# Post-normed products with tokens in the rows: TensorE transposes four blocks ahead of the next products, and four tiles of these run side by side

## The chip, the cores and the metric

One core of one Trainium2 chip runs the whole program. The metric is the device time of one execution in microseconds (us), lower is better; three executions of the kernel before gave a median of 1262.53 us (1261.92 to 1263.29). One more execution was profiled; the rows of the trace are from that one.

## The reference

256 tokens of width 1024 go through two transformer blocks. Only the first block is touched by the change. Cut to what matters:

```python
def first_block(x, mem, ...):
    h = rmsnorm(x, norm_pre_mix)
    z = h @ w_in
    out_a = gmlp_spatial_gating(g_u, g_v, ...)
    out_b = forgetting_attention(f_q, f_k, f_v, log_f)
    out_c = memory_cross_attention(m_q, rmsnorm(mem, norm_mem), w_mem_kv)
    y = concatenate([out_a, out_b, out_c]) @ w_out
    x = x + rmsnorm(y, norm_post_mix)
    h = rmsnorm(x, norm_pre_ffn)
    f = square(relu(h @ w_ff1)) @ w_ff2
    x = x + rmsnorm(f, norm_post_ffn)
    return x

def second_block(x, ...):
    for i in range(2):
        x = x + 0.5 * swiglu(rmsnorm_2(x, ffn_norm1[i]), wg, wu, wd)
        ...
```

The two lines that matter have the form `x = x + rmsnorm(product, gain)`. They are post-norms: the product's root mean square over all 1024 features must be known before any of it can be added to x. The next layer's products need that x. So each of these lines stands between two long runs of matrix products: `w_out` and `w_ff1` in the one case (called the mix transition here), `w_ff2` and the first swiglu's `wg`, `wu` in the other (the feed-forward transition).

## The kernel before, in words

Activations lie transposed: x is eight tiles `x0` to `x7` of 128 features x 256 tokens. Every fp32 product is made of three fp32r matmuls: each operand is split into a rounded part and a rest (`xh`, `xl` for activations, `wh`, `wl` for weights), and `mm_t` (lines 134 to 141) adds `xh*wh` (line 139), `xl*wh` (line 140) and `xh*wl` (line 141) into one PSUM tile. The weight block is the stationary operand, 256 tokens are the moving one, so one output tile of 128 features x 256 tokens from 1024 inputs takes 8 x 3 = 24 matmuls of 256 columns. `mm_n` (lines 143 to 151) does the same with the activations stationary.

The order of work is written out by hand; each engine runs its own list in the order of the program. The class `Stream` (lines 72 to 131) brings the weights: SyncE's queue issues the DMAs of 1 MB into three `raw` tiles, ScalarE rounds a chunk of 1024 columns to `wh` (line 102), VectorE makes the rest `wl` (line 112). There are six pairs of `wh`, `wl`; `get()` keeps four chunks ahead, so a chunk's pair is reused six chunks later.

The mix transition before (lines 796 to 823): the gating of the first mixer part is finished (lines 796 to 809: 12 small matmuls at line 801, VectorE line 804, GpSimd line 808, split lines 212 and 213). `out_proj` makes `y = w_out` product in tiles of 128 features; `y_evac` (lines 483 to 492) squares each on ScalarE, adds the squares up on GpSimd (line 199) and writes `y` times the gain. After the last tile, `norm_cols` (lines 223 to 229) sums the squares over features with matmuls against ones (line 219); VectorE (line 226) and GpSimd (a power of -0.5, line 188) give the factor of each token; since tokens lie in the columns, `diag` (line 234) and a matmul against ones (line 239) spread it over the partitions. `ws.fill()` (lines 126 to 129) splits two more weight chunks in between, the rest of one of them on GpSimd. `post_add` (lines 531 to 546) multiplies and adds the tiles of x one by one (533, 535, two adds on VectorE and six on GpSimd), rounds `xh` on ScalarE (536) and makes `xl` on VectorE (543). Four blocks of small bf16 matmuls for the position bias of a later layer (`t5_mm`, line 522, 24 matmuls each) are put between these steps. Then `ff1` starts with two tiles whose matmuls alternate by input block (lines 846 to 850).

The feed-forward transition before (lines 877 to 899) has the same parts, with the squared norm folded into the factor (lines 888 to 894). It is followed by `ffn2` (lines 388 to 439), whose first tiles run one after another, and whose `start` (lines 925 to 933) makes the squares for the next norm. Steps of the bias (`t5_mask`: GpSimd line 513, VectorE line 515; `t5_evac`: VectorE line 528) are spread over the tiles of `ffn2` as `extra`.

Of the kernel before, what the change touches and what calls it, by code (L numbers as in the profile page):

```python
# [39 lines left out]
N_HOT = 10  # L40

# [9 lines left out]
def block_kernel(ctx: ExitStack, tc: tile.TileContext, a: dict, out: bass.AP, upto: int = 99):  # L51
# [20 lines left out]
    class Stream:  # L72
# [53 lines left out]
        def fill(self):  # L126

            while self.ns < self.ng + HL and self.split(gp):
                pass

# [12 lines left out]
    def mm_n(ps, w, off, n, x, tt, kts, first, last):  # L143
        h, lo = w
        ts = slice(tt * P, tt * P + P)
        for j, (k, kk) in enumerate(kts):
# [4 lines left out]
            pe.matmul(ps, lhsT=x[0][k][:, ts], rhs=lo[:, c:c + n], start=False, stop=s1)  # L151

# [235 lines left out]
    def ffn2(acc, gnext, extra=(), start=None, more=()):  # L388
        extra = list(extra)
        with tc.tile_pool(name="ffa", bufs=1) as fa, tc.tile_pool(name="fft", bufs=2) as ft:  # L390
# [12 lines left out]
            w, w2 = ws.get(), ws.get()  # L403
            p0, p1 = bank(), bank()
            lo7, hi = range(KT - 1), [KT - 1]
            mm_t(p0[:, :T], w, 0, P, X, lo7, True, False)
            mm_t(p1[:, :T], w2, 0, P, X, lo7, True, False)
            if start:
                start()
            mm_t(p0[:, :T], w, 0, P, X, hi, False, True)  # L410
            mm_t(p1[:, :T], w2, 0, P, X, hi, False, True)
            p2 = bank()
            mm_t(p2[:, :T], ws.get(), 0, P, X, range(KT), True, True)
            ms, rs = norm_cols(acc, *more)
            mm_t(p2[:, T:], ws.get(), 0, P, X, range(KT), True, True)
            rb = bcast(rs)
            evac(0, p0[:, :T], p1[:, :T], rb)
            evac(1, p2[:, :T], p2[:, T:], rb)
            for j in range(2, 22):
# [63 lines left out]
    def y_evac(d, p, y, yacc, gi):  # L483

        if d == KT - 1:
            sq = tp.tile([P, T], F32, tag="sq", name="sq")
            act.activation(out=sq, in_=p, func=AF.Square)
        else:
            sq = None
            add_sq(yacc, d, p)  # L490
        act.activation(out=y[d], in_=p, func=AF.Copy, scale=gcol(gi, d))
        return sq
# [38 lines left out]
    def post_add(y, rb, gnext):  # L531
        def add(d):
            dve.tensor_tensor(out=y[d], in0=y[d], in1=rb, op=ALU.mult)
            eng = dve if d < 2 else gp
            eng.tensor_tensor(out=x[d], in0=x[d], in1=y[d], op=ALU.add)
            act.activation(out=xh[d], in_=x[d], func=AF.Copy, scale=gcol(gnext, d))  # L536
            late.append((d, gcol(gnext, d)))

        for d in range(KT):
            add(d)  # L540
            if d > 1:
# [924 lines left out]
```

## Time and profile before

| what | value |
|---|---|
| median of three executions | 1262.53 us (1261.92 to 1263.29) |
| the profiled execution | 1259.43 us |
| span in its trace | 1257.6 us |
| PE (TensorE matmul) busy | 1222.9 us, 97% |
| VectorE (DVE) busy | 846.2 us, 67% |
| ScalarE (ACT) busy | 660.1 us, 52% |
| GpSimd (POOL) busy | 196.1 us, 16% |
| mean granted TensorE clock | 0.989 of full |

The profiled execution took 1259.43 us, of which 1257.6 us are the span of the trace and 1.8 us lie around it. Matmuls are pipelined, so the time of one (0.28 us for 256 columns) is longer than the distance between two that follow each other, and a share of 97% doesn't mean that TensorE is at its peak. Where a stage's work is read, the start of one row is taken from the start of a later one.

### The profile page before, as it was taken

The page shows a single profiled execution, that of the slowest core. Times are in us where ns is not written, and L with a number is a line of the kernel's source. Part 1 is how long each engine was busy: PE and PEld are TensorE (multiplying, and loading weights), DVE is VectorE, ACT ScalarE, POOL GpSimd, SP SyncE. Part 2 cuts the span into 40 slices and gives each one's busy share as a digit, 9 for nine tenths or more (in the row PEclk, how much of TensorE's full clock was granted, in tenths as well). Part 3 has the DMA queues.
Part 4 walks back from the last instruction along what each step waited for, and adds up shares of the span by engine and source line. Part 5 has one row for each costly group of instructions (what it writes and reads, how often), then busy time and mean ns, then how long its engine had stood idle before and what let it go on. Part 6 is the DMA issues. An engine that isn't in the chain of part 4 may idle for free.

```text
span 1257.6 us, 24874 instructions
## 1 busy us (share of the span) xinstructions
PE 1222.9 (97%) x10316; PEld 1187.9 (94%) x10316; DVE 846.2 (67%) x1490; ACT 660.1 (52%) x1174; POOL 196.1 (16%) x192
## 2 busy tenths in 40 slices
PE   8989999999899999999999999999999989999998
PEld 7878899999899999988999999999999869999998
DVE  6886676654677656688766656666566797666553
ACT  5557465444335544577554444545444787545442
POOL 5424210110420001121200001100001462000000
PEclk9999899999899999999999999999999999999999
DMA  7534355655235545631465455555456412555463
GB/s 239 195 104 165 102 201 179 224 193 179 99 132 178 194 153 193 225 135 64 173 202 194 156 183 203 200 171 202 170 170 201 168 68 92 177 193 181 156 203 108
DMA packets 37266, 211.38 MB, mean 168 GB/s; under 512 B 4768, under 2 KB 8224, under 8 KB 18848
## 3 DMA queue, kind: packets, MB, share of 16 engines
q1 hardware_dynamic: 37152, 209.78, 48.9%
q8 instruction: 81, 1.33, 0.4%
q14 instruction: 33, 0.27, 0.1%
HBM read 208.71 MB, written 1.05 MB: 167 GB/s over the span
## 4 chain that ended last, share of the span: by engine, by line
PE 83%; DVE 9%; issue 3%; ACT 2%; DMA 1%; POOL 1%; SPq 0%; ACTq 0%; POOLq 0%; DVEq 0%
PE ps L139 26%; PE ps L140 26%; PE ps L141 25%; DVE wl L112 3%; PE ps L300 1%; PE ps L311 1%; PE ps L332 1%; DMA raw<-in_w1q 1%; PE ps L149 1%; PE ps L150 1%; ACT wh L102 1%; PE ps L151 1%; DVE p L289 1%; ACT p L271 0%; DVE dg L234 0%
## 5 line engine op out<-in xcount | busy, mean ns | idle before, releaser
L139 PE MATMUL ps<-xh,wh 128*128 128x256 f32 (+1 forms) x1848 | 522.0, 282 | 0.5 <-ACT xh L536 0.5
L140 PE MATMUL ps<-xl,wh 128*128 128x256 f32 (+1 forms) x1848 | 519.6, 281 | 1.5 <-DVE xl L543 0.8
L112 DVE TENSOR_TENSOR wl<-raw,wh 128x1024 fp32r<-128x1024 f32 (+3 forms) x434 | 488.7, 1166 | 47.4 <-ACT wh L102 46.9
L141 PE MATMUL ps<-xh,wl 128*128 128x256 f32 (+1 forms) x1848 | 517.9, 280 | 2.5 <-DVE wl L112 2.5
L102 ACT CAST wh<-raw 128x1024 fp32r<-128x1024 f32 (+4 forms) x436 | 400.4, 959 | 63.8 <-PE ps L140 29.7
L140 PEld LDWEIGHTS ps<-xl,wh 128*128 128x128 f32 (+1 forms) x1848 | 348.9, 189 | 3.5 <-DVE xl L543 2.2
L139 PEld LDWEIGHTS ps<-xh,wh 128*128 128x128 f32 (+1 forms) x1848 | 349.3, 189 | 2.8 <-issue 1.7
L141 PEld LDWEIGHTS ps<-xh,wl 128*128 128x128 f32 (+1 forms) x1848 | 349.1, 189 | 2.8 <-DVE wl L112 2.7
L139 PE MATMUL ps<-ah,wh 128*128 128x256 f32 x960 | 267.8, 279 | 0.0
L140 PE MATMUL ps<-al,wh 128*128 128x256 f32 x960 | 267.8, 279 | 0.0
L141 PE MATMUL ps<-ah,wl 128*128 128x256 f32 x960 | 267.8, 279 | 0.0
L139 PEld LDWEIGHTS ps<-ah,wh 128*128 128x128 f32 x960 | 180.4, 188 | 0.0
L140 PEld LDWEIGHTS ps<-al,wh 128*128 128x128 f32 x960 | 180.4, 188 | 0.0
L141 PEld LDWEIGHTS ps<-ah,wl 128*128 128x128 f32 x960 | 180.4, 188 | 0.0
L199 POOL TENSOR_TENSOR acc<-acc,sq 128x256 f32<-128x256 f32 x42 | 49.9, 1189 | 577.6 <-ACT sq L198 577.4
L398 ACT ACTIVATE s<-t 128x256 f32<-128x256 f32 x88 | 36.8, 418 | 191.8 <-DVE t L396 191.8
L396 DVE TENSOR_TENSOR t<-ps,rb 128x256 f32<-128x256 f32 x88 | 37.2, 423 | 73.4 <-PE ps L141 68.1
L213 DVE TENSOR_TENSOR al<-f,ah 128x256 fp32r<-128x256 f32 (+1 forms) x105 | 49.0, 467 | 52.8 <-ACT ah L212 52.8
L212 ACT CAST ah<-f 128x256 fp32r<-128x256 f32 (+1 forms) x105 | 45.9, 437 | 55.8 <-DVE f L400 43.2
L252 ACT ACTIVATE xh<-x,cols 128x256 fp32r<-128x256 f32 x40 | 20.4, 510 | 101.6 <-DVE x L433 94.6
L400 DVE TENSOR_TENSOR f<-ps,s 128x256 f32<-128x256 f32 x88 | 37.4, 425 | 47.4 <-ACT s L398 47.4
L432 DVE SCALAR_TENSOR_TENSOR t<-ps,rb 128x256 f32<-128x256 f32 x32 | 13.6, 425 | 76.9 <-PE ps L141 76.9
(277 smaller groups left out, 1276.3 us busy)
## 6 DMA issues: line engine op xcount, KB each, us to landing
raw<-in_gu SPq DMA_DIRECT2D x88, 1024.0 KB, 4.9
raw<-in_dn SPq DMA_DIRECT2D x64, 704.0 KB, 4.2
raw<-in_ff SPq DMA_DIRECT2D x32, 1024.0 KB, 4.9
raw<-in_w_out SPq DMA_DIRECT2D x4, 1024.0 KB, 4.8
raw<-in_aq SPq DMA_DIRECT2D x4, 1024.0 KB, 4.7
raw<-in_a_out SPq DMA_DIRECT2D x4, 1024.0 KB, 4.8
raw<-in_b_out SPq DMA_DIRECT2D x4, 1024.0 KB, 4.9
raw<-in_w1q SPq DMA_DIRECT2D x6, 512.0 KB, 3.9
```

The costliest lines, as they stand in the source:

```text
L102: act.copy(h[:, :n], t)
L112: eng.tensor_tensor(out=lo, in0=t, in1=h.bitcast(F32), op=ALU.subtract)
L139: pe.matmul(ps, lhsT=h[:, c:c + m], rhs=x[0][k], start=s0, stop=False)
L140: pe.matmul(ps, lhsT=h[:, c:c + m], rhs=x[1][k], start=False, stop=False)
L141: pe.matmul(ps, lhsT=lo[:, c:c + m], rhs=x[0][k], start=False, stop=s1)
L199: gp.tensor_tensor(out=acc, in0=acc, in1=sq, op=ALU.add)
L212: act.copy(h, src)
L213: dve.tensor_tensor(out=lo, in0=src, in1=h.bitcast(F32), op=ALU.subtract)
L252: act.activation(out=xh[k], in_=x[k], func=AF.Copy, scale=gcol(g, k))
L396: dve.tensor_tensor(out=t, in0=g, in1=rb, op=ALU.mult)
L398: act.activation(out=s, in_=t, func=AF.Silu)
L400: dve.tensor_tensor(out=f, in0=u, in1=s, op=ALU.mult)
```

## The change

In the two post-normed products the roles are exchanged: the activations are stationary, the weights are the moving operand in pieces of 512 columns, and the product lies with tokens in the rows (`mm_y`). The sum of squares of a token is then a sum along the free axis, which ScalarE gives with its accumulator (`y_sq`), and the factor is one scalar per partition (`y_rstd`), which ScalarE (tokens 0 to 127) and VectorE (tokens 128 to 255) multiply on while they bring the product out of PSUM (`y_scale`). TensorE transposes blocks of 128 features back into PSUM, one VectorE instruction multiplies by the gain and adds to x, and `prep` rounds (`PostAdd.turn`). `PostAdd.products` runs four tiles of the next layer's products side by side: for each input block k, two more blocks are transposed (until all eight are), then 12 matmuls use block k. `fill`, the spreading matmul of the factor, GpSimd's adds to x and the sums of squares over tiles on GpSimd go. In the mix transition the gating (12 small matmuls and what follows) moves behind the first three input blocks of the `w_out` product. The squares for the next norm are made in `turn`; `ffn2` takes the four tiles as `begun`, and makes its next factor's diagonal on ScalarE instead of VectorE.

```diff
+MIX_ORDER = [3, 4, 5, 6, 7, 0, 1, 2]
-        def fill(self):
-            while self.ns < self.ng + HL and self.split(gp):
-                pass
+    def mm_y(banks, w, n, x, kts, first, last):
+        for tt in range(2):
+            for j in range(len(banks[tt])):
+                h, lo = w
+                ts = slice(tt * P, tt * P + P)
+                for i, k in enumerate(kts):
+                    c = (i * len(banks[tt]) + j) * n
+                    s0, s1 = first and i == 0, last and i == len(kts) - 1
+                    ps = banks[tt][j][:, :n]
+                    pe.matmul(ps, lhsT=x[0][k][:, ts], rhs=h[:, c:c + n], start=s0, stop=False)
+                    pe.matmul(ps, lhsT=x[1][k][:, ts], rhs=h[:, c:c + n], start=False, stop=False)
+                    pe.matmul(ps, lhsT=x[0][k][:, ts], rhs=lo[:, c:c + n], start=False, stop=s1)
...
+    def y_sq(ps, ss, tt, h, junk):
+        act.activation(out=junk, in_=ps, func=AF.Square, accum_out=ss[:, h, tt:tt + 1])
+    def y_rstd(ss, eps):
...
+        dve.scalar_tensor_tensor(out=ms, in0=ss[:, 1], scalar=1.0 / D, in1=s0, op0=ALU.mult, op1=ALU.add)
+        rs = sm.tile([P, 2], F32, tag="rs", bufs=3, name="rs")
+        rstd_pow(rs, ms, 2)
+        return rs
+    def y_scale(ps, y, rs, pieces):
+        for h, o, n in pieces:
+            src = [ps[tt][h][:, o:o + n] for tt in range(2)]
+            dst = [y[tt][:, 512 * h + o:512 * h + o + n] for tt in range(2)]
+            act.activation(out=dst[0], in_=src[0], func=AF.Copy, scale=rs[:, 0:1])
+            dve.tensor_scalar(out=dst[1], in0=src[1], scalar1=rs[:, 1:2], scalar2=None, op0=ALU.mult)
+    class PostAdd:
...
+        def turn(self):
...
+            ps = bank()
+            for tt in range(2):
+                pe.transpose(ps[:, tt * P:tt * P + P], self.y[tt][:, d * P:d * P + P], ident)
+            dve.scalar_tensor_tensor(out=x[d], in0=ps[:, :T], scalar=gcol(self.gi, d), in1=x[d], op0=ALU.mult, op1=ALU.add)
+            prep(d, self.gnext, self.acc)
...
+        def products(self, outs, w):
+            for k in range(KT):
+                self.turn()
+                self.turn()
+                for i, (p, wi) in enumerate(zip(outs, w)):
+                    mm_t(p, wi, 0, P, X, [k], k == 0 and i % 2 == 0, k == KT - 1 and i % 2 == 1)
+                if k in (2, 4):
+                    ws.split()
+                    ws.low()
...
+        py = [[bank() for _ in range(2)] for _ in range(2)]
+        for i, k in enumerate(MIX_ORDER):
+            if i == 3:
+                gmlp_out()
+                warm_table(AF.Silu)
+            if i < KT - 2:
+                mm_y(py, ws.get(), 512, (oh, ol), [k], i == 0, False)
...
+        t5 = [t5_mm([o5[:, i]]) for i in range(3)]
+        rs_y = y_rstd(ss, None)
+        y_scale(py, y, rs_y, ((0, 0, T), (0, T, T)))
+        acc = new_acc()
+        add = PostAdd(y, 1, 2, acc)
+        add.turn()
+        add.turn()
+        y_scale(py, y, rs_y, ((1, 0, 2 * T),))
+        t5.append(t5_mm([o5[:, 3]]))
+        w = [ws.get(AHEAD - 1 - i) for i in range(4)]
+        p = [bank() for _ in range(2)]
+        add.products([b[:, o:o + T] for b in p for o in (0, T)], w)
...
-            p = bank()
-            for k0 in range(0, 32, 8):
-                mm_t(p[:, :T], ws.get(), 0, P, (AH[k0:], AL[k0:]), range(8), k0 == 0, k0 == 24)
-            ysq = y_evac(d, p[:, :T], ys, yacc, 3)
+        for h in range(2):
+            for i in range(16):
+                if h == 0 and i % 4 == 0:
+                    t5_mask(4 + i // 4, n5, o5[i // 4])
+                mm_y([[py[tt][h]] for tt in range(2)], ws.get(), 512, (AH, AL), [2 * i, 2 * i + 1], i == 0, i == 15)
...
+            if begun:
+                p = bank()
+                mm_t(p[:, :T], ws.get(), 0, P, X, range(KT), True, True)
+                _, rs = norm_cols(acc)
...
+                mm_t(p[:, T:], ws.get(), 0, P, X, range(KT), True, True)
+                rb = bcast(rs, dg=dg)
+                for j, p in enumerate(begun + [p]):
+                    evac(j, p[:, :T], p[:, T:], rb)
```

The weights of `w_out` and `w_ff2` are laid out for this on the way in; their bytes and the number of DMAs stay the same.

How the change moves instructions is seen best at three places. The first is TensorE's list behind the last matmuls of the attention units (line 332, 342 in the change), where the gating's matmuls (801, 851) stand. `oh`, `ol` are the mixers' outputs. Before:

```order
L332 MATMUL ps<-pt,vm_178 64x256 x2
L332 MATMUL ps<-pt,vm_179 64x256 x2
L801 MATMUL ps<-wst,gv_174 64x128
...
L801 MATMUL ps<-wst,gv_175 64x128
L139 MATMUL ps<-oh_183,wh_1146 128x256
```

In the change, three input blocks of 12 matmuls stand ahead of them (the last three and the first three of what follows are shown):

```order
L159 MATMUL ps<-wh_1243,oh_185 128x512
L160 MATMUL ps<-wh_1243,ol_193 128x512
L161 MATMUL ps<-wl_1244,oh_185 128x512
L851 MATMUL ps<-wst,gv_174 64x128
...
L851 MATMUL ps<-wst,gv_175 64x128
L159 MATMUL ps<-wh_1279,oh_186 128x512
L160 MATMUL ps<-wh_1279,ol_194 128x512
```

The gating moved from ahead of the `w_out` product to behind 36 of its matmuls.

The second is TensorE's list between the last matmul of the `w_out` product and the first of `ff1`. `o` is the bias step's mask, `macc` and `sq` the sums of squares, `dg` the diagonal, `kon` holds ones and the identity. Before:

```order
L141 MATMUL ps<-oh_182,wl_1487 128x256
L522 LDWEIGHTS o_1011
...
L219 MATMUL ps<-kon,macc 128x1
L219 MATMUL ps<-kon,sq 128x1
...
L239 MATMUL ps<-dg,kon 128x256
...
L139 MATMUL ps<-xh_89,wh_1503 128x256
L140 MATMUL ps<-xl_97,wh_1503 128x256
L141 MATMUL ps<-xh_89,wl_1504 128x256
L139 MATMUL ps<-xh_89,wh_1543 128x256
```

In the change (587 are the bias matmuls, 542 the transposes, 135 to 137 the lines of `mm_t`):

```order
L161 MATMUL ps<-wl_1416,oh_182 128x512
L587 LDWEIGHTS o_1004
...
L542 MATMUL ps<-kon,y 128x128 x4
L587 LDWEIGHTS o_1004
...
L542 MATMUL ps<-kon,y 128x128 x4
L135 MATMUL ps<-xh_89,wh_1431 128x256
L136 MATMUL ps<-xl_97,wh_1431 128x256
...
L137 MATMUL ps<-xh_89,wl_1472 128x256
L542 MATMUL ps<-kon,y 128x128 x4
L135 MATMUL ps<-xh_90,wh_1431 128x256
```

The matmuls for the sum and the spread went; 16 transposes came, four at a time, the last four two input blocks behind the first products; block 0 (`xh_89`) is used by four weight tiles before block 1 (`xh_90`).

The third is VectorE's list at the same place. Before:

```order
L226 TENSOR_SCALAR ms<-ps 128x2
L234 TENSOR_SCALAR dg<-kon,rs 128x128 x2
L533 TENSOR_TENSOR y_1366<-y_1366,ps 128x256
L535 TENSOR_TENSOR x_81<-x_81,y_1366 128x256
L533 TENSOR_TENSOR y_1367<-y_1367,ps 128x256
L535 TENSOR_TENSOR x_82<-x_82,y_1367 128x256
L533 TENSOR_TENSOR y_1368<-y_1368,ps 128x256
L543 SCALAR_TENSOR_TENSOR xl_97<-x_81,cols,xh_89 128x256
```

In the change:

```order
L516 SCALAR_TENSOR_TENSOR ms<-ss,s_1585 128x2
L526 TENSOR_SCALAR y<-ps,rs 128x256 x2
L543 SCALAR_TENSOR_TENSOR x_81<-ps,cols,x_81 128x256
L543 SCALAR_TENSOR_TENSOR x_82<-ps,cols,x_82 128x256
L271 SCALAR_TENSOR_TENSOR xl_97<-x_81,cols,xh_89 128x256
L526 TENSOR_SCALAR y<-ps,rs 128x512
L543 SCALAR_TENSOR_TENSOR x_83<-ps,cols,x_83 128x256
L271 SCALAR_TENSOR_TENSOR xl_98<-x_82,cols,xh_90 128x256
```

The diagonal went, the multiplication moved in front of the transposes, and one instruction now does what a multiplication and an addition did.

## Rows read from the trace of the kernel before

**Rows 1.** The page, the chain of work that ended last, shares by engine.
```profile
PE 83%; DVE 9%; issue 3%; ACT 2%; DMA 1%; POOL 1%; SPq 0%; ACTq 0%; POOLq 0%; DVEq 0%
```

**Rows 2.** Waits of PE, 84 to 150 us, then 150 to 345 us (total, times, longest).
```profile
PE ps L239 <- DVE dg L234: 2.2, 1, 2.2
PE ps L801 <- POOL gv L790: 1.8, 2, 1.4
...
PE ps L239 <- DVE dg L234: 2.7, 1, 2.7
```

**Rows 3.** PE in order of time, mix transition (start, us, engine, line, operation).
```profile
105.09 0.43 PE L801 MATMUL ps<-wst,gv 128*64 128x128 f32 x2 [1.41 <-POOL gv L790]
105.88 1.53 PE L801 MATMUL ps<-wst,gv 128*64 128x128 f32 x22 [0.36 <-POOL gv L790]
...
129.86 0.87 PE L522 MATMUL ps<-rbd,o 128*128 128x64 bf16 x24
...
131.46 1.56 PE L522 MATMUL ps<-rbd,o 128*128 128x64 bf16 x48
...
145.92 0.28 PE L139 MATMUL ps<-xh,wh 128*128 128x256 f32 x1
```

**Rows 4.** PE in order of time, feed-forward transition.
```profile
319.98 0.87 PE L522 MATMUL ps<-rbd,o 128*128 128x64 bf16 x24
...
328.05 0.58 PE L139 MATMUL ps<-xh,wh 128*128 128x256 f32 x1 [0.23 <-ACT xh L536]
...
347.00 0.47 PE L139 MATMUL ps<-xh,wh 128*128 128x256 f32 x1
```

**Rows 5.** DVE and POOL in order of time behind the factors' powers.
```profile
131.88 0.71 POOL L188 TENSOR_TENSOR rs<-ms,mhalf 128x2 f32<-128x2 f32 x1 [3.28 <-DVE ms L226]
132.56 2.34 POOL L112 TENSOR_TENSOR wl<-raw,wh 128x1024 fp32r<-128x1024 f32 x1
...
322.94 2.30 DVE L894 TENSOR_TENSOR fy<-fy,r 128x2 f32<-128x2 f32 x1 [0.82 <-POOL fy L188]
```

**Rows 6.** Windows: length, busy (x) of PE, PEld, DVE, ACT, POOL, PEclk, DMA, GB/s.
```profile
140.00:142.00 2.00, 2.00 (x11) 2.00 (x11) 2.00 (x6) 1.03 (x3) 2.00 (x3) 0.50 0.00 0
...
326.00:328.00 2.00, 1.82 (x26) 1.52 (x25) 1.35 (x4) 0.51 (x1) 0.00 (x0) 0.59 0.00 0
...
336.00:338.00 2.00, 2.00 (x17) 2.00 (x17) 1.79 (x4) 0.92 (x4) 1.83 (x3) 0.85 0.03 8
```

**Rows 7.** PE in order of time: 512-column matmuls, and 256-column ones later.
```profile
1006.12 0.39 PE L149 MATMUL ps<-wh,ch 128*128 128x512 f32 x1
1006.35 0.39 PE L150 MATMUL ps<-wh,cl 128*128 128x512 f32 x1
...
142.07 0.28 PE L139 MATMUL ps<-xh,wh 128*128 128x256 f32 x1
```

**Rows 8.** Groups by line and shape: xcount, busy us, mean ns, idle before.
```profile
L841 ACT ACTIVATE t<-ps 128x512 f32<-128x512 f32 x15 | 9.0, 598 | 23.4 <-PE ps L141 23.4
L271 ACT ACTIVATION_READ_ACCUMULATOR p<-s,nm 128x1 f32 x44 | 8.3, 189 | 0.0
L491 ACT ACTIVATE y<-ps,cols 128x256 f32<-128x256 f32 x16 | 7.6, 475 | 0.0
L311 PE MATMUL ps<-kon,p 128*128 128x128 f32 x130 | 22.7, 282 | 8.2 <-DVE p L289 7.9 <-ACT pt L314 0.3
L432 DVE SCALAR_TENSOR_TENSOR t<-ps,rb 128x256 f32<-128x256 f32 x32 | 13.6, 425 | 76.9 <-PE ps L141 76.9
L536 ACT ACTIVATE xh<-x,cols 128x256 fp32r<-128x256 f32 x16 | 8.1, 508 | 15.1 <-DVE x L535 9.9 <-POOL x L535 5.3
L543 DVE SCALAR_TENSOR_TENSOR xl<-x,cols,xh 128x256 fp32r<-128x256 f32 x12 | 6.9, 572 | 0.0
```

**Rows 9.** VectorE in `ffn2`, then waits of PE, 345 to 395 us.
```profile
372.10 4.06 DVE L112 TENSOR_TENSOR wl<-raw,wh 128x1024 fp32r<-128x1024 f32 x2
...
PE ps L522 <- DVE o L515: 1.7, 2, 0.9
```

More of the change, by code (lines that the diff above doesn't have):

```diff
@@ L385, in warm_table, with ffn2 @@
         act.activation(out=t, in_=mhalf[:, 0:1], func=func)
-    def ffn2(acc, gnext, extra=(), start=None, more=()):
+    def ffn2(acc, gnext, extra=(), begun=None):
         extra = list(extra)
@@ L602, in block_kernel @@
         mem = [mem_[:, k] for k in range(KT)]
-        mh = [mp.tile([P, T], F32R, tag=f"mh{k}", name=f"mh{k}") for k in range(KT)]
+        mh_ = mp.tile([P, KT, T], F32R, tag="mh", name="mh")
+        mh = [mh_[:, k] for k in range(KT)]
         ml_ = mp.tile([P, KT, T], F32R, tag="ml", name="ml")
@@ L812, in block_kernel, with gmlp_out @@
-        yacc = new_acc("macc")
-        ysq = []
-        ys = [mp.tile([P, T], F32, tag=f"mh{k}", name=f"y{k}") for k in range(KT)]
-        out_proj(pipe, oh, ol, [[3, 4, 5, 6, 7], [0, 1, 2]], lambda d, p: ysq.append(y_evac(d, p, ys, yacc, 1)))
-        t5 = [t5_mm([o5[:, 0]])]
-        _, rs_y = norm_cols(yacc, ysq[-1])
-        t5 += [t5_mm([o5[:, i]]) for i in (1, 2)]
-        dg = diag(rs_y)
-        ws.fill()
-        rb = bcast_ps(dg)[:, :T]
+        def gmlp_out():
+            for j in range(3):
+                pm = bank()
+                for g in (2 * j, 2 * j + 1):
+                    r = slice(64 * (g % 2), 64 * (g % 2) + 64)
+                    for tt in range(2):
+                        pe.matmul(pm[r, tt * P:tt * P + P], lhsT=gv[tt][:, 64 * g:64 * g + 64], rhs=wst[:, g, :],
+                                  start=True, stop=True)
+                t = tp.tile([P, T], F32, tag="t", name="t")
+                dve.scalar_tensor_tensor(out=t.rearrange("p (c t) -> p c t", c=2), in0=pm[:, :T].rearrange("p (c t) -> p c t", c=2),
+                                         scalar=cols[:, C_GV + j:C_GV + j + 1],
+                                         in1=bsb[:, j:j + 1, :].to_broadcast([P, 2, P]), op0=ALU.mult, op1=ALU.add)
+                f = tp.tile([P, T], F32, tag="f", name="f")
+                gp.tensor_tensor(out=f, in0=t, in1=uT[j], op=ALU.mult)
+                split_plain(oh[j], ol[j], f)
@@ new lines, in block_kernel @@
+        while not pipe.done():
+            pipe.step()
+        y_ = mp.tile([P, 2, D], F32, tag="mh", name="y")
+        y = [y_[:, tt] for tt in range(2)]
+        ss = sm.tile([P, 2, 2], F32, tag="ss", name="ss")
+        py = [[bank() for _ in range(2)] for _ in range(2)]
[5 more added lines that the diff above has]
+                mm_y(py, ws.get(), 512, (oh, ol), [k], i == 0, False)
@@ L898, in block_kernel @@
+        t5 = [t5_mm(o5[i]) for i in range(3)]
+        rs_y = y_rstd(ss, eps)
+        y_scale(py, y, rs_y, ((0, 0, T), (0, T, T)))
+        acc = new_acc()
+        add = PostAdd(y, 3, g2("ffn_norm1_2", 0), acc)
+        add.turn()
+        add.turn()
+        y_scale(py, y, rs_y, ((1, 0, 2 * T),))
         t5.append(t5_mm(o5[3]))
-        acc = post_add(ys, rb, g2("ffn_norm1_2", 0))
+        w = [ws.get(AHEAD - 1 - i) for i in range(4)]
+        p = [bank() for _ in range(2)]
+        add.products([b[:, o:o + T] for b in p for o in (0, T)], w)
@@ L912, in f @@
                 def f():
-                    if t5 and j > 8:
+                    if t5:
                         t5_evac(*t5.pop(0))
@@ L921, in t5_step @@
                 return f
[L923 to L935 removed]
+            acc = ffn2(acc, g2("mix_norm_2", 0), [t5_step(j) for j in range(4, 16)], p)
         if upto == 3:
```

169 lines of the change are left out of this document (62 added, 107 removed), and 2 rows, old and new, of the table seq.

## The prediction

> **What bounds the kernel now.** I read the chain of work that ended last first: 83% of it is TensorE [rows 1], so only two things can make the program shorter: fewer or cheaper matmuls, or less time in which TensorE stands still or runs at half clock. Next I looked for those stretches around the two post-norms, in the waits of TensorE [rows 2]. Three are there: 1.8 us before the gating's matmuls (GpSimd is still scaling `gv`), and 2.2 and 2.7 us before the matmul that spreads the factor. Then I read TensorE's rows in order of time. In the mix transition the last `y` matmul is followed at 129.86 by bias matmuls, and the first two `ff1` tiles (48 matmuls) are done only at 145.92 [rows 3]. In the feed-forward transition the last `y` matmul is followed at 319.98, products start at 328.05, and at 347.00 TensorE has done four tiles (96 matmuls), the next norm's sum and its spreading [rows 4].
>
> Two causes of these long stretches show in other views. GpSimd's part of `fill`, a weight rest of 2.34 us, starts as the power ends, and a two-element VectorE instruction beside such a one took 2.30 us [rows 5]. And the granted clock was 0.50 (1.2 GHz, half of the upper level) at 140 to 142 us and 0.59 on average at 326 to 328; it was still 0.85 on average at 336 to 338 [rows 6], although TensorE had been fed again since 328.05. So the wait costs twice: once as idle time, once as slow matmuls behind it.
>
> **The change, part by part.** E is the time at which the last `y` matmul makes room for the next instruction.
>
> *The products themselves: nothing.* 768 matmuls of 256 columns become 384 of 512, 192 become 96. Matmuls of 512 columns start 0.23 us apart (1006.12, 1006.35), and 33 of 256 columns lie between 142.07 [rows 7] and 145.92 [rows 3], 0.117 us apart, which is half. The columns cost the same either way, and I take 0. The Trainium skill ("TensorE: Matmul & The Clock Gate", Back-to-back issue gap) has a fixed 2.5 ns in each matmul; by that the 480 matmuls saved would give 1.2 us. The rows show no such gain.
>
> *The gating behind 36 matmuls of the `w_out` product: -1.8 us.* The two waits of 1.41 and 0.36 us [rows 3] end when GpSimd has scaled `gv`. Now 8.4 us of products (36 x 0.233) that need nothing of the gating lie ahead. What comes behind it (VectorE, GpSimd, two splits, three times) has two more input blocks, 5.6 us, to hide under. If these weights came late, the wait would stay and the gain be 0.
>
> *The mix transition, E to 96 matmuls done.* Before: 145.92 - 129.86 = 16.1 us to 48 matmuls [rows 3], and 48 more at 0.117 are 5.6: 21.7 us. After, step by step, with durations from [rows 8] unless another group is named:
> - the sum of squares: the nearest ScalarE row over 512 PSUM columns takes 0.60, the accumulator's read 0.19; with 0.2 for the end of the last matmul, E+1.0;
> - the mean on VectorE, 0.3 (0.42 lie between 131.46 and the power's start at 131.88, and hold the end of a matmul too [rows 3, 5]), and the power, 0.71 [rows 5]: E+2.0;
> - `y` times the factor, 256 columns out of PSUM, 0.48: E+2.5;
> - two transposes: a transpose row has 0.28, the second I put 0.12 behind like a 256-column matmul: E+2.9;
> - the gain and the addition, like the VectorE row of 0.43; `xh` 0.51; `xl` 0.57; 0.2 for three hand-overs: first full set of operands at E+4.65.
>
> Under this chain lie three sets of bias matmuls (0.75 us each, half of the row of 48 less its tail [rows 3]), the transposes of two blocks and the fourth set: 3.8 us of work in 4.65, so TensorE idles 0.9 us, and no gap is longer than half a us. Then 96 matmuls take 11.2 us, the transposes of blocks 4 to 7 some 1.0, and 0.3 goes because transposes alternate between two PSUM banks and wait for VectorE to empty them: E+17.1. VectorE's pace is 0.43 + 0.57 = 1.0 us for a block, ScalarE's two operations of about 0.5, `xh` and the square; TensorE needs 1.4 for the 12 matmuls of one, so they keep ahead. The bounds: without any wait 3.0 + 1.9 + 11.2 = 16.1; with every transpose at its full 0.28 and a wait of 0.4 us in each later turn, 20. I take 17.1: **-4.6 us**.
>
> *The feed-forward transition, up to 96 matmuls, the next norm's sum and its spreading.* Before 347.00 - 319.98 = 27.0 us [rows 4]. After: the same chain, 17.1, then the sum's four half-matmuls 0.4 and the spreading 0.4, as the next factor is now made under one tile half of 2.8 us: 17.9. **-9.1 us**. It is larger than the other since half clock lasted longer and a second wait behind the next factor goes with it.
>
> *What is late next: +1.5 us.* Four weight chunks are held until the side-by-side tiles end, and six pairs exist, so only two chunks are ready behind them. In the mix transition VectorE has to square, split two evacuations and add a bias block before the third rest, due 5.8 us after the products; I count 6.1, a wait of 0.3. In `ffn2` three evacuations come at once and put VectorE some us behind; four steps later the bias masks slow it, when GpSimd makes two rests take 4.06 us, and TensorE already waits 1.7 us there now [rows 9]. With less slack I count 2.9, so 1.2 more. The ends are 0 and 4.
>
> *Nothing:* DMAs, equal in number and bytes, on the same queue, which is ahead by whole chunks; the squares for the next norm, which fill ScalarE beside products (without that cover 0.5 us a block); the removed adds on GpSimd.
>
> The sum: -1.8 - 4.6 - 9.1 + 1.5 = -14.0 us. From the profiled execution's 1259.4 this gives 1245.4. That execution lies 3.1 us below the median of the three shown, which is what the result is set against, so I forecast 1262.5 - 14.0 = **1248.5 us**.
>
> **The rivals.**
>
> *The clock falls once more.* For it: between E and E+4.65 TensorE has thin work, and in both transitions before the clock fell soon after the bias matmuls. Against it: the gaps were then over 2 us, now they are below 0.5. If it stays at half as long as before, 6.7 and 10 us, each us costs half of one: up to 8 us, 1257; in one transition alone 1252 to 1254.
>
> *VectorE becomes the bound behind the tiles.* It catches up slowly, since its work fills most of the 5.6 us (48 x 0.117) that two tiles take. If the first rests come two instructions later than I count, 2 to 2.5 us go in each place: 1253.
>
> *Slower: half clock through all side-by-side products.* The mechanism is the transposes between the products: they come in groups of four ahead of the first three blocks, after a thin stretch, and the clock stays at half until the last tile. The rows show it can last while TensorE is busy: 2.00 of 2.00 us at a clock of 0.50 [rows 6]. 96 matmuls at half clock cost at most 11.2 us more, in two places 22.4: 1271. It decides in favour of slower from 28 us of half clock in the two together, twice the 14.0 gained. The rule of the Trainium skill that speaks for it ("TensorE: Matmul & The Clock Gate", Part 4: PE-mode transpose) says the full clock does not engage for transposes. Against it: from the fourth block on there are no transposes, and 60 matmuls in a row brought the clock back before.
>
> *The wait only moves.* If weight rests or VectorE set the pace of the whole stretch, TensorE would idle later by what it saves: 1262. Against it: none of TensorE's waits around the two transitions [rows 2] is for `wl`.
>
> **How the numbers follow.** Forecast 0.60, clock 0.22, VectorE 0.09, half clock throughout 0.05, moved wait 0.04. The forecast's own bounds run from 1244 (no wait in the chain, 2 us, and nothing late, 1.5) to 1254; the range must also take in most of the clock's case: 1244 to 1257. A change of 0.2% (2.5 us, about what a measurement of this kernel can tell from none) divides the cases: faster than 1260.0 are the first three, 0.89 with a piece of doubt for three errors in one direction; the same 0.06; slower 0.05.
>
> **What would show it.** Right: PEclk stays at 1.00 from E on in both transitions; the first products start about 4.7 us behind the bias matmuls' start, and 96 matmuls end 17 us behind it; no wait in front of the gating's matmuls; 512-column matmuls 0.23 us apart. Wrong: a granted clock of 0.50 in the transposed products, transposes waiting on VectorE at every block, or TensorE waiting for `wl` longer than 1.5 us in the tiles that follow.

## The result and the profile after

The changed kernel takes 1244.65 us (median of four executions, 1239.26 to 1249.46) against 1262.51 us before: a ratio of 0.9863, interval 0.9841 to 0.9885, 17.9 us less. The forecast was 1248.5, 14.0 us less. The profiled execution is the slowest of the four, 1249.46 us with a span of 1247.7.

The page's chain of work that ended last, shares by engine, answers to [rows 1]: TensorE still bounds the kernel, and the 1% of GpSimd is gone.

```profile
PE 84%; DVE 10%; ACT 3%; issue 2%; DMA 1%; POOL 0%; SPq 0%; ACTq 0%; DVEq 0%
```

TensorE in order of time in the mix transition, answering to [rows 3]; columns as there, the idle time and what ended it in brackets:

```profile
117.43 1.58 PE L851 MATMUL ps<-wst,gv 128*64 128x128 f32 x24
...
133.04 2.27 PE L587 MATMUL ps<-rbd,o 128*128 128x64 bf16 x72
135.51 0.80 PE L542 MATMUL ps<-kon,y 128*128 128x128 f32 x4 [0.20 <-ACT y L525]
136.15 0.86 PE L587 MATMUL ps<-rbd,o 128*128 128x64 bf16 x24
136.85 0.63 PE L542 MATMUL ps<-kon,y 128*128 128x128 f32 x4
138.34 0.35 PE L135 MATMUL ps<-xh,wh 128*128 128x256 f32 x1 [0.86 <-DVE y L526]
...
150.74 0.28 PE L135 MATMUL ps<-xh,wh 128*128 128x256 f32 x1
```

E is 133.04. The gating (851) waits for nothing, products start at E+5.30, and the 97th matmul of the side-by-side tiles starts at 150.74, so 96 are done at E+17.7. The same view of the feed-forward transition, answering to [rows 4]:

```profile
319.61 2.27 PE L587 MATMUL ps<-rbd,o 128*128 128x64 bf16 x72
...
324.87 0.36 PE L135 MATMUL ps<-xh,wh 128*128 128x256 f32 x1 [0.86 <-DVE y L526]
...
337.26 0.28 PE L135 MATMUL ps<-xh,wh 128*128 128x256 f32 x1
...
343.32 0.64 PE L249 MATMUL ps<-dg,kon 128*128 128x256 f32 x2
344.46 0.39 PE L135 MATMUL ps<-xh,wh 128*128 128x256 f32 x1 [0.50 <-ACT rb L255]
```

Windows (columns as in [rows 6]) of the transitions, and one of the unchanged beginning:

```profile
133.00:138.00 5.00, 4.29 (x105) 3.71 (x104) 2.86 (x7) 3.02 (x9) 0.69 (x1) 1.00 0.85 352
138.00:142.00 4.00, 3.65 (x30) 3.50 (x30) 3.67 (x9) 3.05 (x8) 2.40 (x3) 1.00 0.02 4
319.00:325.00 6.00, 4.99 (x109) 4.18 (x108) 3.34 (x8) 3.59 (x11) 1.08 (x2) 1.00 0.25 105
325.00:329.00 4.00, 3.99 (x34) 3.75 (x35) 3.67 (x8) 3.02 (x9) 2.75 (x4) 1.00 0.02 4
41.00:55.00 14.00, 14.00 (x57) 12.09 (x56) 10.32 (x19) 5.72 (x11) 6.20 (x7) 0.51 0.53 173
```

The clock is 1.00 (2.4 GHz) through both transitions, transposes included. But at 41 to 55 us, in code that the change leaves alone, it was 0.51 in this execution. The two traces by stage, each from the start of one matmul to the start of another:

| stage | before | after | difference |
|---|---|---|---|
| start to the last attention matmul | 103.3 | 108.5 | +5.2 |
| from there to E | 26.6 | 24.5 | -2.0 |
| E to 96 matmuls of `ff1` done | 21.7 | 17.7 | -4.0 |
| from there to E of the feed-forward transition | 168.5 | 168.9 | +0.4 |
| E to 144 matmuls done, factor spread | 32.8 | 24.9 | -8.0 |
| rest of `ffn2` to its down products | 111.7 | 111.1 | -0.6 |
| from there to the end | 793.1 | 792.2 | -1.0 |

The five stages in the middle give -14.2 us; the forecast's sum for them was -14.0. The 5.2 us at the start stand beside 17.1 us at half clock where the other execution had 6.8, in unchanged code; what else took part there stays open. The last stage needs the experiments: it runs no line that was changed, and yet its matmuls have other distances.

### The profile page after: what moved, and what is told of

Same layout as the page of the kernel before. It is cut to its first block, busy times and chain, and to the rows that moved or that the text cites. A ratio compares the mean times of both kernels' runs of the same rounds, so it can differ in the third digit from the quotient of the medians.

```text
span 1247.7 us, 23873 instructions
## 1 busy us (share of the span) xinstructions
PE 1221.4 (98%) x9844; PEld 1165.4 (93%) x9844; DVE 840.4 (67%) x1482; ACT 658.1 (53%) x1164; POOL 175.6 (14%) x169
## 4 chain that ended last, share of the span: by engine, by line
PE 84%; DVE 10%; ACT 3%; issue 2%; DMA 1%; POOL 0%; SPq 0%; ACTq 0%; DVEq 0%
PE ps L135 23%; PE ps L137 23%; PE ps L136 23%; DVE wl L113 3%; PE ps L159 3%; PE ps L161 3%; PE ps L160 3%; PE ps L310 1%; PE ps L342 1%; PE ps L321 1%; DVE p L299 1%; DMA raw<-in_w1q 1%; PE ps L145 1%; PE ps L146 1%; ACT wh L103 1%
## 5 line engine op out<-in xcount | busy, mean ns | idle before, releaser
L113 DVE TENSOR_TENSOR wl<-raw,wh 128x1024 fp32r<-128x1024 f32 (+4 forms) x436 | 491.2, 1165 | 57.1 <-ACT wh L103 56.7
L137 PE MATMUL ps<-ah,wl 128*128 128x256 f32 x704 | 195.7, 278 | 0.0
L136 PE MATMUL ps<-al,wh 128*128 128x256 f32 x704 | 195.4, 278 | 0.0
L135 PE MATMUL ps<-ah,wh 128*128 128x256 f32 x704 | 195.4, 278 | 0.0
L136 PEld LDWEIGHTS ps<-al,wh 128*128 128x128 f32 x704 | 132.3, 188 | 0.0
L137 PEld LDWEIGHTS ps<-ah,wl 128*128 128x128 f32 x704 | 132.2, 188 | 0.0
L135 PEld LDWEIGHTS ps<-ah,wh 128*128 128x128 f32 x704 | 131.9, 187 | 0.0
L209 POOL TENSOR_TENSOR acc<-acc,sq 128x256 f32<-128x256 f32 x49 | 55.2, 1127 | 516.7 <-ACT sq L208 516.2
L262 ACT ACTIVATE xh<-x,cols 128x256 fp32r<-128x256 f32 x56 | 28.5, 509 | 105.9 <-DVE x L454 94.6
```

What stands on the lines that cost most here:

```text
L113: eng.tensor_tensor(out=lo, in0=t, in1=h.bitcast(F32), op=ALU.subtract)
L135: pe.matmul(ps, lhsT=h[:, c:c + m], rhs=x[0][k], start=s0, stop=False)
L136: pe.matmul(ps, lhsT=h[:, c:c + m], rhs=x[1][k], start=False, stop=False)
L137: pe.matmul(ps, lhsT=lo[:, c:c + m], rhs=x[0][k], start=False, stop=s1)
L209: gp.tensor_tensor(out=acc, in0=acc, in1=sq, op=ALU.add)
```

## The experiments

All medians stand beside the kernel before on the same chip (1260.6 to 1261.2 us). Since executions differ by some us at the start, the stages of each trace carry the verdicts.

**The gating ahead of the products again.**

```diff
+            if i == 0:
+                gmlp_out()
             if i == 3:
-                gmlp_out()
                 warm_table(AF.Silu)
```

> The changed kernel with one part undone: the gating stands ahead of the w_out product again. Theory (the gating's matmuls wait for GpSimd's scaled gv unless products lie ahead): 1.4 to 1.9 us of waiting return in front of the gating's matmuls, and the stretch from the last attention matmul to E, the end of the y product, goes from 24.5 to 26.3 us or a little more; everything behind E stays (E to 96 matmuls 17.7 us, and 24.9 us to 144 matmuls in the feed-forward transition). Rival (the shorter stretch comes from the wider matmuls, not from the order): it stays at 24.5 us.

1241.45 us (0.9848, 0.9819 to 0.9877). TensorE around the gating:

```profile
103.95 0.43 PE L851 MATMUL ps<-wst,gv 128*64 128x128 f32 x2
104.73 1.53 PE L851 MATMUL ps<-wst,gv 128*64 128x128 f32 x22 [0.35 <-POOL gv L839]
```

The wait is back, but as 0.35 us, and the stretch to E is 25.0 us, 0.5 more than with the gating moved. Neither number expected came out. What the move is worth depends on the execution: of traces with the gating first, two have 26.6 and 26.7 us there and four 25.0 to 25.2, while the eight with the gating moved all have 24.5 or 24.6.

**No bias matmuls between E and the products.**

```diff
-        t5 = [t5_mm([o5[:, i]]) for i in range(3)]
         rs_y = y_rstd(ss, None)
...
-        t5.append(t5_mm([o5[:, 3]]))
...
         add.products([b[:, o:o + T] for b in p for o in (0, T)], w)
+        t5 = [t5_mm([o5[:, i]]) for i in range(4)]
```

(and the same in the other transition)

> The changed kernel with the four blocks of bias matmuls moved behind the side-by-side products in both transitions, so that TensorE has only the transposes between E and the first products. Theory A (the thin work keeps the clock up, and that is most of the gain): TensorE idles some 4.4 us of the 5.3 us before the first products, the granted clock falls to 0.50 for 3 to 10 us in one or both transitions, E to 96 matmuls goes from 17.7 to 19.4 to 22 us, and with the 3.0 us of bias work that now comes later each place loses 4.7 to 7 us, 10 to 14 us in all. Theory B (the clock does not care about this gap): the clock stays at 1.00, E to 96 matmuls stays at 17.7 us, and only the bias work is added, 3.0 us in each place, 6 us in all.

1248.39 us (0.9900, 0.9881 to 0.9920). TensorE, and two windows:

```profile
129.40 0.39 PE L161 MATMUL ps<-wl,oh 128*128 128x512 f32 x1
132.11 1.09 PE L542 MATMUL ps<-kon,y 128*128 128x128 f32 x8 [2.32 <-ACT y L525]
133.66 0.58 PE L135 MATMUL ps<-xh,wh 128*128 128x256 f32 x1 [0.46 <-ACT xh L262]
...
147.52 2.97 PE L587 MATMUL ps<-rbd,o 128*128 128x64 bf16 x96
```

```profile
132.00:136.00 4.00, 3.43 (x17) 2.96 (x18) 3.69 (x9) 3.30 (x9) 0.74 (x1) 0.70 0.49 199
136.00:138.00 2.00, 2.00 (x16) 2.00 (x15) 1.25 (x4) 1.08 (x4) 1.66 (x2) 0.76 0.00 0
```

Here E is 0.23 behind the start of the last `y` matmul, 129.63. Half of each theory holds. The clock fell, for 3.4 us in each transition (2 x (0.30 x 4 + 0.24 x 2) in the windows). But 96 matmuls were done at 147.52, E+17.9, nearly as in the changed kernel (17.7), and behind them come the bias matmuls, 2.8 us. Two things cancel in the 17.9. The products started at E+4.03, not 5.30, and waited for `xh`, not for `y`. And from there the 96 took 13.9 us, 12.4 in the changed kernel (138.34 to 150.74); in the other transition, 14.2 and 12.4. So 3.4 us of half clock cost 1.5 and 1.8 us, about half of its length, since TensorE waits for no block in these products. The bias blocks keep the clock up, but they also hold the first products back by about what that saves, and what is left as their gain is their own time.

**Two pairs, and one tile alone, in place of four side by side.**

```diff
-                for i, (p, wi) in enumerate(zip(outs, w)):
-                    mm_t(p, wi, 0, P, X, [k], k == 0 and i % 2 == 0, k == KT - 1 and i % 2 == 1)
+                for i in range(2):
+                    mm_t(outs[i], w[i], 0, P, X, [k], k == 0 and i % 2 == 0, k == KT - 1 and i % 2 == 1)
+            for k in range(KT):
+                for i in range(2, 4):
+                    mm_t(outs[i], w[i], 0, P, X, [k], k == 0 and i % 2 == 0, k == KT - 1 and i % 2 == 1)
-                if k in (2, 4):
+                if k in (0, 3):
                     ws.split()
                     ws.low()
```

The two weight splits move into the last loop. In the second run the loop with the transposes holds tile 0 alone, and a loop for tile 1 stands ahead of the one for tiles 2 and 3.

> The changed kernel with the four tiles run in two pairs: the first two follow the transposed blocks, the other two come behind them. Theory (VectorE makes a block in 0.9 to 1.0 us, TensorE uses one up in 0.83 us with its transposes when two tiles run, in 1.5 when four do): TensorE waits 0.1 to 0.2 us at most blocks, and E to 96 matmuls goes from 17.7 to 18.5 to 20 us in each transition. Rival (the width carries the gain, as two tiles are what the kernel before ran): 3 us or more in each transition.

> The changed kernel with the first of the four tiles run alone, block by block as they are transposed, and the other three behind it. Pairs cost nothing (17.77 and 17.59 us from E to 96 matmuls against 17.69 and 17.65). Theory (VectorE makes a block in some 0.95 us; one tile uses it up in 0.35 and a transposed block's share of 0.13): TensorE waits about 0.45 us at each of the last six blocks, and E to 96 matmuls takes 20 to 21 us in each transition, 5 to 7 us in all. Rival (the first block's arrival is all that counts): 17.7 us stay.

Pairs: 1240.22 us (0.9834, 0.9815 to 0.9853), E to 96 matmuls 17.8 and 17.6 us; no block was waited for. Both sides of that expectation miss: two tiles are wide enough, so running four side by side is no part of the gain over pairs. One alone: 1245.51 us (0.9870, 0.9850 to 0.9890), E to 96 matmuls 20.2 and 20.1 us, so 2.5 and 2.4 us more. Of its waits of TensorE in the mix transition (total, times, longest), those for `xl` and `x` are new and show VectorE behind:

```profile
PE ps L136 <- DVE xl L271: 0.9, 3, 0.4
PE ps L135 <- DVE y L526: 0.9, 1, 0.9
PE ps L542 <- DVE x L543: 0.3, 1, 0.3
```

**The kernel before with its idle time filled.**

```diff
         ws.fill()
+        spin(9, o5[:, 0, 0:4])
         rb = bcast_ps(dg)[:, :T]
         t5.append(t5_mm([o5[:, 3]]))
+        spin(5, o5[:, 0, 0:4])
```

(`spin` issues bf16 matmuls of 512 columns into a bank that nothing reads; the same in the other transition)

> The kernel before, with idle time filled: 9 bf16 matmuls of 512 columns that nothing reads ahead of the matmul that spreads the factor, and 5 more behind the fourth block of bias matmuls, in both transitions. Theory (half of the lost time is half clock that the idle time brings on: 6.8 and 10.2 us at half clock in the profiled execution): the granted clock stays at 1.00, E to 96 matmuls in the mix transition goes from 21.7 to about 18.3 us, and E to 144 matmuls in the feed-forward transition from 32.8 to about 27.7 us, 8.5 us in all. Rival (what counts is the wait chain, and the slow matmuls lie under it): both stretches stay within 1 us, or grow by the fillers that don't fit.

1260.01 us (0.9997, 0.9982 to 1.0011). E is 128.54; TensorE, and the windows:

```profile
128.54 0.87 PE L527 MATMUL ps<-rbd,o 128*128 128x64 bf16 x24
...
131.76 1.89 PE L386 MATMUL ps<-o 128*128 128x512 bf16 x8
133.92 0.70 PE L239 MATMUL ps<-dg,kon 128*128 128x256 f32 x2 [0.27 <-DVE dg L234]
...
149.44 0.28 PE L139 MATMUL ps<-xh,wh 128*128 128x256 f32 x1
```

```profile
129.00:136.00 7.00, 6.68 (x109) 4.81 (x107) 4.00 (x7) 2.85 (x5) 3.02 (x2) 1.00 0.45 152
...
326.00:336.00 10.00, 8.02 (x53) 6.62 (x53) 9.21 (x20) 6.60 (x16) 7.63 (x9) 1.00 0.01 2
```

The clock stayed at 1.00 where before it was 0.50 and 0.59 [rows 6], and E to 96 matmuls is 20.9 us (21.7 before), E to 144 in the other transition 31.8 (32.8). Keeping the clock up is worth 0.8 and 1.1 us here, not 3.4 and 5.1, half of the 6.8 and 10.2 at half clock: at full clock TensorE only waits longer for the next block (8.02 busy of 10).

**The kernel before without `fill`.**

```diff
         dg = diag(rs_y)
-        ws.fill()
         rb = bcast_ps(dg)[:, :T]
```

> The kernel before without the two calls of fill, so that no weight rest runs on GpSimd while VectorE makes the factor and its diagonal; the two chunks that fill rounded early are rounded when they are asked for. Theory (the rest on GpSimd holds VectorE up: two diagonal halves took 2.56 us beside it in one place, the two-element product 2.30 us in the other, where 0.5 and 0.2 us are usual): E to the first products goes from 8.1 to about 6.0 us in both transitions, nearly as far as the change brings it (5.3), E to 96 matmuls from 21.7 to 19.6 us and E to 144 matmuls in the feed-forward transition from 32.8 to 30.7 us, less what the weights then come late, 0 to 2 us in each: 0 to 4 us in all. Rival (the spreading matmul and the two VectorE instructions of each block behind it are what costs): less than 0.7 us at the first products.

1255.90 us (0.9963, 0.9945 to 0.9980). First two lines of the kernel before: VectorE's diagonal in the mix transition, and GpSimd's rest beside the two-element product of the other.

```profile
132.62 2.56 DVE L234 TENSOR_SCALAR dg<-kon,rs 128x128 f32<-128x128 f32 x2 [0.82 <-POOL rs L188]
...
322.88 2.34 POOL L112 TENSOR_TENSOR wl<-raw,wh 128x1024 fp32r<-128x1024 f32 x1
```

Without `fill` E is 128.83; TensorE and VectorE in the mix transition, then VectorE in the other:

```profile
128.83 0.87 PE L522 MATMUL ps<-rbd,o 128*128 128x64 bf16 x24
...
131.59 0.48 DVE L234 TENSOR_SCALAR dg<-kon,rs 128x128 f32<-128x128 f32 x2 [0.82 <-POOL rs L188]
...
134.34 0.38 PE L139 MATMUL ps<-xh,wh 128*128 128x256 f32 x1 [0.81 <-ACT xh L536]
...
147.67 0.28 PE L139 MATMUL ps<-xh,wh 128*128 128x256 f32 x1
...
319.08 0.16 DVE L893 TENSOR_TENSOR fy<-fy,r 128x2 f32<-128x2 f32 x1 [0.82 <-POOL fy L188]
```

The diagonal takes 0.48 where it took 2.56, and the two-element instruction 0.16 where it took 2.30 beside GpSimd's rest [rows 5]. Products start at E+5.5 and E+5.9 (8.1 before), E to 96 matmuls is 18.8, and E to 144 in the other transition 30.2. In the mix transition this one deletion brings 2.8 of the change's 4.0 us, in the other 2.6 of 8.0; in the mix transition the clock stayed at 1.00 too, so the 2.8 hold what that is worth. The Trainium skill ("SBUF — State Buffer", Who interferes with whom) says that VectorE and GpSimd share a pair of ports, that this pair is an exclusive lock, and that a VectorE instruction with two inputs in SBUF contends for it with a GpSimd instruction that reads SBUF. The trace agrees: the two-element product starts at 322.94, in GpSimd's 2.34 us, and ends at 325.24, as that does (325.22).

**Tiles moved by 32 bytes and more.** The change replaces three small tiles by four, so all tiles behind them, the swiglus' activations `ah`, `al` among them, start 32 bytes further on. Six runs move tiles and change nothing else, by an unused tile among the small ones (`pad`: 8 columns in the first three runs, 56 in the fourth and fifth) and by the gap ahead of x (`fill`: taken out in the third, 16 columns in the fourth and sixth). The fourth, for one:

```diff
-    lead2.tile([P, 8], F32, name="fill")
+    lead2.tile([P, 16], F32, name="fill")
...
+    sm.tile([P, 56], F32, name="pad")
```

> The kernel before with nothing changed but an unused tile of 32 bytes per partition among the small tiles, which moves all tiles behind it by 32 bytes, as the changed kernel's new small tiles do by chance. Theory (the place of the moving operand sets the distance of matmuls): the four stretches of 528 matmuls that read the activations of the swiglus, 61.49 us each in the kernel before (116.67 ns from one to the next), fall to 59.73 us (113.34 ns) in two to four of them, as in the changed kernel's trace, so 3.5 to 7 us are won without any other change. Rival (those stretches are shorter for a reason that lies in the change's order of work): they stay at 61.49 us and the time stays at 1261 to 1262 us.

> The changed kernel with the same unused tile of 32 bytes, which brings the swiglus' activations back to addresses that are multiples of 64. Theory (the place of the moving operand): all four stretches of 528 matmuls take 61.49 us or more again, and the time rises by 3.5 to 7 us over the changed kernel's other executions, to about 1246 to 1249 us. Rival (the order of work): two to four of them stay at 59.73 us and the time at 1240 to 1245 us.

> The changed kernel with the 32-byte gap ahead of the residual tiles taken out and put behind the small tiles, so that x, xh and xl lie 32 bytes beside a multiple of 64, like the weights' tiles and the swiglus' activations. Theory (what counts is where the moving operand lies against 64 bytes): the long stretches of products that read xh and xl, 116.7 ns from one to the next, fall to 113.3 ns too, 3%: of some 670 us about 19 us, so 1222 to 1228 us. Rival (only the swiglus' stretches can run at the shorter distance, as they read 22 tiles once each in a row): 116.7 ns stay, and the time is the changed kernel's, 1239 to 1246 us. A third way: the engines that make xh and xl, or read x, get slower at such addresses, and the time rises.

> The changed kernel with the gap ahead of the residual tiles made 64 bytes instead of 32, and 224 unused bytes among the small tiles: x, xh and xl start at 32 past a multiple of 256 bytes, the swiglus' activations too. The runs so far give, by the place of the moving operand past a multiple of 256 bytes with the weights at 224: 0: 116.7 ns; 32: 113.3 (117.8 in some stretches); 64: 120.0; 224: 119.9. Theory (the place of the moving operand against the weights' sets the distance): the products that read xh and xl fall from 116.7 to 113.3 ns; 5688 of them are 19 us, so 1221 to 1228 us. Rival (x at any place other than 0 is worse, as at 224, for what else reads and writes it): 117 to 120 ns, 1245 to 1265 us.

> The changed kernel with 224 unused bytes among the small tiles, which put the swiglus' activations at a multiple of 256 bytes as in the kernel before, so that the change is compared without the move of its tiles. Theory (the change's order of work is worth some 14 us: 2.0 in front of the end of the y product, 4.0 and 8.0 in the two transitions; the rest of the 17.9 us was the place of tiles): the four stretches of 528 matmuls take 61.49 us each as before, and the time is 1245 to 1249 us. Rival (the place of tiles counts for more, since it took 9.5 us to move them by 32 bytes): 1250 us or more. Second rival (the whole gain is the order's): 1240 to 1244 us.

> The kernel before with the gap ahead of the residual tiles made 64 bytes instead of 32: x, xh, xl and the swiglus' activations all start at 32 past a multiple of 256 bytes. Theory (place of the moving operand): 116.7 to 113.3 ns in the products of both kinds, 7 us in the swiglus' four stretches, 2.6 us in w_ff2's product and some 19 us in the others, so 1231 to 1238 us, and the changed kernel with the same places stays some 12 to 14 us below it. Rival: as for the run with both at 32, the products that read xh and xl don't gain, and 1250 to 1257 us come out.

Windows of 40 us in the down products of the third swiglu: the kernel before, the same with 32 bytes more, the changed kernel, the same with 32 more (one fence for each):

```profile
920.00:960.00 40.00, 40.00 (x345) 40.00 (x344) 25.60 (x36) 18.00 (x30) 4.95 (x4) 1.00 0.60 197
```

```profile
920.00:960.00 40.00, 40.00 (x356) 40.00 (x355) 26.05 (x38) 18.52 (x33) 4.96 (x4) 1.00 0.59 199
```

```profile
920.00:960.00 40.00, 40.00 (x356) 40.00 (x354) 26.93 (x37) 19.00 (x32) 6.37 (x5) 1.00 0.60 200
```

```profile
920.00:960.00 40.00, 40.00 (x336) 40.00 (x335) 25.45 (x35) 18.19 (x30) 6.34 (x5) 1.00 0.55 186
```

At the same granted clock of 1.00 TensorE gets 345, 356, 356 and 336 matmuls into 40 us. The stretch of 528 there takes 61.49, 59.73, 59.73 and 63.24 us from first start to last: 116.7, 113.3, 113.3 and 120.0 ns. By the place past a multiple of 256 bytes:

| kernel | x, xh, xl at | ah, al at | xh, xl products (three stretches of 960), ns | four stretches of 528, us | median, us (ratio to before) |
|---|---|---|---|---|---|
| before | 0 | 0 | 116.7 | 61.49 four times | 1260.6 |
| before, +32 | 0 | 32 | 116.7 | 59.73 four times | 1256.64 (0.9962) |
| change | 0 | 32 | 117.8 once, 116.7 twice | 62.07 twice, 59.73 twice | 1244.65 (0.9863) |
| change, ah at 0 | 0 | 0 | 117.8 once, 116.7 twice | 62.07 twice, 61.49 twice | 1247.76 (0.9891) |
| change, +32 | 0 | 64 | 116.7 | 63.24 four times | 1254.19 (0.9955) |
| change, x moved back | 224 | 32 | 120.0 | 62.07 four times | 1264.11 (1.0030) |
| change, both at 32 | 32 | 32 | 117.8 | 62.07 four times | 1252.81 (0.9931) |
| before, both at 32 | 32 | 32 | 117.8 | 62.07 four times | 1269.18 (1.0065) |

The place of tiles alone moves the time by -4 us (kernel before, +32) and +9.5 us (changed kernel, +32), and with x at 224 it eats the whole gain. My rule for it, that the place of the moving operand against the weights' sets the distance, fell: with x at 32 no product got faster, and `ah` at 32 no longer gave 59.73 us. The expectations fared accordingly: the kernel before with 32 bytes more, the changed kernel with `ah` at 0 (its time, but two stretches took 62.07 us) and the rival of the changed kernel with both at 32 came out; the changed kernel with 32 more lost more than expected, with x moved back it took the third way, and the kernel before with both at 32 missed both sides. Nor does the place alone decide: the kernels before with fillers and without `fill` have all these tiles where the kernel before has them, and one of their four stretches took 62.07 us; the changed kernel's layout gave 59.73 four times in the runs with the gating first and with one tile alone.

With `ah` and x where the kernel before has them, the change is worth 13.2 us (0.9891, 0.9872 to 0.9911), close to the 14.0 forecast; with both kernels' `ah` at 32, 12.0 us (1256.64 to 1244.65), and with x and `ah` at 32 in both, 16.4 (1269.18 to 1252.81).

No run here is shown to beat the changed kernel: the gating first and the pairs have medians 3 to 4 us lower, inside the spread of its own executions.

## Why the prediction was right, and where it wasn't

**What bounds it.** That only the stretches around the post-norms could be gained was right: the five middle stages hold 14.2 us of difference. **"So the wait costs twice: once as idle time, once as slow matmuls behind it" failed for most of the second cost.** With the clock held at 1.00 the kernel before gains 0.8 and 1.1 us. The rest of its slow matmuls lay under the chain of blocks from VectorE, GpSimd and ScalarE, and would otherwise have been waits. The price is right where no block is waited for: 3.4 us of half clock cost the changed kernel without bias blocks 1.5 and 1.8 us. `fill`, which the prediction named beside it, was the larger cause in the mix transition (2.8 of 4.0 us).

**The gating, -1.8.** Measured -2.0 between the profiled executions, but 0.5 when undone alone. The term was the wait of one execution, and that wait varies from 0.35 to 1.8 us; that the result has it in full is luck.

**The mix transition, -4.6: measured -4.0.** The step that failed is to let the products start with the "first full set of operands at E+4.65". VectorE and ScalarE in order of time:

```profile
136.51 0.51 ACT L262 ACTIVATE xh<-x,cols 128x256 fp32r<-128x256 f32 x1 [0.68 <-DVE x L543]
```

```profile
137.05 0.48 DVE L271 SCALAR_TENSOR_TENSOR xl<-x,cols,xh 128x256 fp32r<-128x256 f32 x1 [0.18 <-ACT xh L262]
137.45 0.75 DVE L526 TENSOR_SCALAR y<-ps,rs 128x512 f32<-128x512 f32 x1
```

The operands were complete at 137.53, E+4.5, so that size was right, but the first product started at 138.34, behind the 512-column evacuation that ends at 138.20. I followed its operands and not the place it writes to: `y` holds four of the eight PSUM banks, the bias blocks and two transposes need six more, so its bank must be one that `y` leaves. The profile has no bank numbers, but names this evacuation as what ended the wait, and without bias blocks the first product started at E+4.03. From there on the forecast holds: 12.4 us to the 97th matmul, 12.45 forecast (17.1 less 4.65).

**The feed-forward transition, -9.1: measured -8.0.** Besides a start of the products that is 0.6 late here too (E+5.26), the sum and spreading of the next factor were put at 0.8 us and take 1.5: 0.37 for the sum (340.06 to 340.43), and 343.32 to 344.46, with a wait of 0.50 behind the spreading. The reason given for the larger gain, half clock lasting longer, accounts for at most the 1.1 us of the fillers' run. Of the 8.0 us, 2.6 come with `fill` gone. The other parts are argued, not shown one by one: a first tile that runs alone costs some 2.4, if the kernel before loses by it what the changed one does; the rest is a shorter chain to the first block (5.9 to 5.3), the shorter sum and wait of the next factor, and the clock's 1.1.

**Late next, +1.5: measured -0.2** (+0.4 and -0.6). Behind the tiles TensorE waited 0.2 us for `wl` between 150 and 420 us, and 0.6 for the bias masks, which cost 1.7 before [rows 9].

```profile
PE ps L587 <- DVE o L580: 0.6, 1, 0.6
PE ps L135 <- ACT rb L255: 0.5, 1, 0.5
```

I let VectorE lose slack by what it was given, and not win it back by what left it (`fill`'s holds, the diagonals, the multiplications); no run tests that reason.

**What the sum had no term for** is the move of tiles. "The products themselves: nothing" holds for the two that were changed (512 columns start 0.23 us apart, 109.41 and 109.64), but other products changed their distance. With the activations at the old place 4.7 us less are won than measured (13.2 against 17.9), of which 3.1 lie between the two changed kernels' medians (1247.76, 1244.65) and 1.6 between those of the kernel before in the two comparisons (1260.95, 1262.51). So the forecast of 14.0 fits the order of work, which was worth 12.0 to 16.4 us at equal places, and in the median the place of tiles makes the result larger.

**Luck.** The 14.0 came out because errors cancel: the two transitions gave 1.7 us less than forecast, and the late work 1.7 less than it was to cost. The measured 1244.65 lies just inside the range, whose lower end rests on a slip of mine: 1248.5 less 2 and 1.5 is 1245.0, not the 1244 that I took as the forecast's lower bound.

**The rivals.** The clock did not fall: in the two transitions TensorE was idle for 0.9 us at most at a stretch. The transposes did not hold it at half: it was 1.00 in all four windows. The Trainium skill ("TensorE: Matmul & The Clock Gate", Part 4: PE-mode transpose) has no full clock for transposes; these windows, in which they alternate with other matmuls, don't agree with that, and no run here shows a longer stretch of transposes alone. My argument against this rival, that 60 matmuls in a row had brought the clock back, misread the trace: 15 and 30 product matmuls had started when it returned (137.97 to 142.0, 328.05 to 336.6). VectorE did not become the bound, and the wait did not move.

## What to carry to other kernels

Before calling slow matmuls a cost, ask whether the next one would have had its operands at full clock; filling the idle time tests it in one run. Look for a GpSimd instruction beside a short VectorE one on the chain, since deleting one may give most of what a new layout gives, and follow a first product to its PSUM bank as well as to its operands. When an edit adds or drops a tile, compare it once with all tiles back in their old places, because here up to 1.6% came from addresses alone (1244.65 to 1264.11 us).

## What the runs showed of the hardware

- Moving tiles by 32 bytes changed the distance of 256-column fp32r matmuls, at a granted clock of 1.00, between 113.3, 116.7, 117.8 and 120.0 ns. What decides between them stays open: one execution of the changed kernel had 59.73 us in two and 62.07 us in two of its four equal stretches, and two runs with unmoved tiles had one stretch of 62.07 beside three of 61.49.
- 14 bf16 matmuls that nothing reads, in each transition, kept the clock at 1.00 through stretches in which it had been at 0.50 and 0.59, and the kernel's time stayed the same (0.9997).
- With the bias matmuls taken out, TensorE stood still for 2.3 us, the clock was at half for 3.4 us in each transition, and 96 product matmuls that wait for no block took 13.9 and 14.2 us where they take 12.4.
- A two-element VectorE instruction took 2.30 us beside a GpSimd instruction of 2.34 us, and 0.16 without it.
- Half clock in the unchanged beginning, up to the last attention matmul, lasted from 3.4 to 20.5 us in the traces, and the beginning took 102.4 us with 3.4 and 108.7 with 20.5; two traces with 6.8 took 103.3 and some 106, so half clock isn't all of it. Filling its waits was not tried.
